# Forming the four weight sums of a seven-product down projection in DRAM, during the attention stages, instead of beside the products

## The chip, the cores and the metric

The kernel runs on one core of a Trainium2 chip. The metric is the device time of one execution in microseconds (us), lower is better. The kernel before took 995.37 us, the median of three runs (993.64 to 995.89).

## The reference, cut to what matters

One layer of a hybrid diffusion backbone on 512 latent tokens (D = 1024) with 256 context tokens. Modulated RMSNorm, a combined input projection, a short convolution branch, a bidirectional gated linear attention of four heads, sigmoid gates, an output projection, then a squared-ReLU MLP, a residual add and a last RMSNorm:

```python
sh1, sc1, ga1, sh2, sc2, ga2 = jnp.split(mod_lat, N_MOD, axis=-1)   # silu(c) @ w_ada + b_ada
o_lat = gla_bidir(ql, kl, vl, gfl, gbl, s_f, s_b)
y_lat = mixer_merge(x_a, b_a, c_a, r, gate_a, gate_b, o_lat, ...)
x = x + ga1 * (y_lat @ w_o)
x = x + ga2 * sq_relu_mlp(modulate(x, g_norm2, sh2, sc2), w_up, w_down)   # square(relu(h @ w_up)) @ w_down
return rmsnorm(x, g_final)
```

The change is about `w_down` alone: a 512x4096 matrix times a 4096x1024 one.

## The kernel before, in words

Everything is fp32. A matmul is made of three fp32r products (`mm3`): each operand is split into a high part (a cast on ScalarE) and a low part (a subtract on VectorE, `split`). Weights are streamed in tiles of 128x1024 (512 KB): `weights()` takes one of four `raw` buffers (NRAW), loads it by SyncE's queue, and splits it into `hi` and `lo`, five buffers each. `Stream` runs a plan of all weight tiles, three ahead of their use: v, q, then x_a, c, b (and q) for the convolution branch, ga, co, r, gb, go, wo, up and dn. The names of tiles follow: `r_co` is the raw tile, `h_co` and `l_co` its parts, `ps_co` the PSUM tile.

The stages: keys and the first modulation, then `projections()`, whose 57 steps are interleaved one by one with the steps of the attention of the four heads (`all_attention`), to about 453 us; `gates()` (r and gb, eight steps each); go, wo and up; from 815.4 us the down projection; then the last norm.

`second_mods()` sums the remaining modulation rows (`ada_sum`): eight loads of `w_ada` (tile `wa`, 512 KB, in the same four raw buffers) for one row of 1024, two `scalar_tensor_tensor` into `acc` on VectorE for each. It runs beside the projection steps from step MODS_FROM = 44 on, and beside the gates. `ada_rows` then splits the sum (`ah`, `al`) and spreads it over the partitions by matmuls into `ps_ar`.

The down projection is a seven-product scheme of Strassen's kind. The 4096x1024 weights are four quarters, `quarter(j, hf, p)`: half j of the rows, half hf of the columns, in eight tiles p. Product n takes eight blocks of 12 matmuls: a left part (`left_parts`: `aph`, `apl` from `ug`) and a weight tile. Four of the seven weights are sums of quarters. Before, tiles p of the sums stand in SBUF (`t_raw`, in four `big` buffers): product 1 loads quarter (0,0) there and splits it; products 2, 3 and 6 each add one more quarter on top of the same tile by an accumulating DMA on GpSimd's queue (`added`, L1056), after the split of the product before. Products 0, 4 and 5 use the raw ring: 0 and 4 a plain load, 5 a plain load (L1064) and then an accumulating DMA on top of it in the same raw tile.

GpSimd's queue also sets a few constants and loads: `lrf` and `lpb` memsets in each head (L610, L611), the v bias `vb` (L802), `acc` memsets and bias rows (L725, L726), `g` (L766). SyncE's queue holds the weight loads, in the plan's order, and the stores of the output rows.

Of the kernel before, what the change touches and what calls it, by code (L numbers as in the profile page):

```python
# [8 lines left out]
F32 = mybir.dt.float32  # L9
F32R = mybir.dt.float32r  # L10
# [3 lines left out]
ALU = mybir.AluOpType  # L14

P = 128
# [15 lines left out]
NFF = D_FF // P  # L32
# [7 lines left out]
NBLK = 36  # L40
NKEEP = 16
MODS_FROM = 44
UP_ORDER = [16 * j + 4 * g + i for g in range(4) for j in range(2) for i in range(4)]
TABLES = "natural_log_exp_and_others"

# [2 lines left out]
def hybrid_block_kernel(  # L48
# [6 lines left out]
    nc = tc.nc  # L55
    x, ctx, w_ada, w_in = x[0], ctx[0], w_ada[0], w_in[0]
    conv_w, w_conv_out, w_gla_out, w_o = conv_w[0], w_conv_out[0], w_gla_out[0], w_o[0]
    w_up, w_down, b_in, b_ada, out = w_up[0], w_down[0], b_in[0], b_ada[0], out[0]

    const = es.enter_context(tc.tile_pool(name="const", bufs=1))  # L60
    wp = es.enter_context(tc.tile_pool(name="wp", bufs=NW))
    kp = es.enter_context(tc.tile_pool(name="kp", bufs=NKEEP))
    sp = es.enter_context(tc.tile_pool(name="sp", bufs=4))
    pp = es.enter_context(tc.tile_pool(name="pp", bufs=8, space=bass.MemoryType.PSUM))

    bp = tc.alloc_tile_pool(name="bp", bufs=NBLK)

# [23 lines left out]
    def kblk(name, dt=F32):  # L91
        return kp.tile([P, 512], dt, tag="kb", name=name)

    def big(name):

        t = [kp.tile([P, 4, 512], F32R, tag="big", name=f"{name}_{i}", bufs=4) for i in range(2)]
        return t, [t[k // 4][:, k % 4, :] for k in range(KT)]
# [4 lines left out]
    def raw_tile(name):  # L102
        return wp.tile([P, 1024], F32, tag="raw", name=name, bufs=NRAW)

    def pinned(ins):
        tc.keep_in_program_order(ins)

    def split(src, hi, lo):
        act.copy(out=hi, in_=src)
        dve.tensor_tensor(out=lo, in0=src, in1=hi.bitcast(F32), op=ALU.subtract)  # L110

    def parts_of(name, src):
        got = blk(name + "h", F32R), blk(name + "l", F32R)
        split(src, *got)
        return got

    def weights(name, src):

        raw = raw_tile("r_" + name)
        a, b = src.shape[1], src.shape[2]  # L120
        nc.sync.dma_start(out=raw.rearrange("p (a b) -> p a b", a=a), in_=src)
        hi = wp.tile([P, 1024], F32R, tag="hi", name="h_" + name)
        lo = wp.tile([P, 1024], F32R, tag="lo", name="l_" + name)
        split(raw, hi, lo)
        return hi.rearrange("p (a b) -> p a b", a=a), lo.rearrange("p (a b) -> p a b", a=a)

    def parted(name, src):

        hi = wp.tile([P, 1024], F32R, tag="hi", name="h_" + name)
        lo = wp.tile([P, 1024], F32R, tag="lo", name="l_" + name)  # L130
        split(src, hi, lo)
        return hi.rearrange("p (a b) -> p a b", a=2), lo.rearrange("p (a b) -> p a b", a=2)

    def mm3(ps, lh, ll, rh, rl, start, stop, late=False, more=False):


        pe.matmul(ps, lh, rh, start=start, stop=False, skip_group_check=more)
        for l, r in ((ll, rh), (lh, rl)) if late else ((lh, rl), (ll, rh)):
            pe.matmul(ps, l, r, start=False, stop=stop and r is (rl if late else rh), skip_group_check=more)
# [4 lines left out]
    def rows(w, k0, c0):  # L144
        return w[k0 * P:(k0 + 2) * P, c0:c0 + 512].rearrange("(k p) c -> p k c", p=P)
# [49 lines left out]
    for m in range(MT):  # L195
        t = (kblk(f"x_{m}_0"), kblk(f"x_{m}_1"))
# [6 lines left out]
    def key_raw(k):  # L203
        wr = blk(f"wk_{k}")
        nc.sync.dma_start(out=wr, in_=w_in[k * P:(k + 1) * P, C_K:C_K + 512])
        return wr
# [91 lines left out]
    def constants():  # L298

        ps = psum("ps_vb")  # L300
        pe.transpose(out=ps[:, 0:97], in_=vec_b, identity=ident[:97, :97])
        dve.tensor_copy(out=col_b, in_=ps[:, 0:97])

        a2h, a2l = blk("a2h", F32R), blk("a2l")
        act.copy(out=a2h, in_=a2)
        dve.tensor_tensor(out=a2l, in0=a2, in1=a2h.bitcast(F32), op=ALU.subtract)
        dve.tensor_scalar(out=a2l, in0=a2l, scalar1=m_2, scalar2=None, op0=ALU.mult)
        dve.scalar_tensor_tensor(out=a2s, in0=a2h.bitcast(F32), scalar=m_01, in1=a2l, op0=ALU.mult, op1=ALU.add)
# [13 lines left out]
    _, h_hi = big("hh")  # L322
    _, h_lo = big("hl")
# [61 lines left out]
    for s in range(2):  # L385
        dve.tensor_copy(out=lr_sel[:, 64 * s:64 * s + 48].rearrange("p (i r) -> p i r", i=3),
                        in_=sel[:, 16 * s:16 * s + 16].unsqueeze(1).to_broadcast([P, 3, RANK]))
# [35 lines left out]
    for k in range(KT):  # L423
        if k == 3:
            constants()
        if k + 2 < KT:
            key_raws[k + 2] = key_raw(k + 2)
            mod_w[k + 2] = [ada_raw(k + 2, q) for q in range(2)]
            key_weights(k + 2)
        elif k + 2 == KT:  # L430
            for m in range(MC):
                t = (blk(f"c_{m}_0"), blk(f"c_{m}_1"))
                for hf in range(2):
                    nc.sync.dma_start(out=t[hf], in_=ctx[m * P:(m + 1) * P, hf * 512:(hf + 1) * 512])
                c_tok.append(t)
        st, sp_ = k == 0, k == KT - 1
        if k % 4 == 3:
            low_rank_products(ps_lr, h_f32, k - 3)
        if k == KT - 1:
            lr_parts = low_rank_parts(ps_lr, SEQ)  # L440
        for h in range(HEADS):
            if h == 0 and k + 1 < KT:
                sm = mod_rows(k + 1)
            if h == 2 and k + 1 < KT:
                with tc.high_priority(offset=60):
                    mod_cols(k + 1, sm)
                    latent_h(k + 1)
            mm3(ps_k[h], wk[k][0][:, h * P:(h + 1) * P], wk[k][1][:, h * P:(h + 1) * P], h_hi[k], h_lo[k], st, sp_, st)
        mm3(ps_q0, wq[0][:, k, :], wq[1][:, k, :], h_hi[k], h_lo[k], st, sp_)

    class Stream:

# [31 lines left out]
    plan += [("wo", rows(w_o, 2 * g, 512 * hf)) for hf in range(2) for g in range(KT // 2)]  # L484
    plan += [("up", cols(w_up, f * P)) for f in UP_ORDER]
    plan += [("dn", lambda n=n, p=p: down_weights(n, p)) for n in range(7) for p in range(NFF // 4)]
# [263 lines left out]
    def all_attention():  # L750
        for h in range(HEADS):
            yield from attention(h)
# [3 lines left out]
    def second_mods():  # L756
        yield from ada_sum(3)
        ps = psum("ps_ac")
        for k in range(KT):
            pe.matmul(ps[:, k:k + 1], ada[3][k // 4][:, (k % 4) * P:(k % 4 + 1) * P], ones[:, 0:1], start=True, stop=True)  # L760
        dve.tensor_copy(out=sh2, in_=ps[:, 0:KT])
        yield
        yield from ada_rows(4)
        for hf in range(2):
            g2 = blk("g2")
            nc.gpsimd.dma_start(out=g2, in_=g_norm2[0][hf * 512:(hf + 1) * 512].partition_broadcast(P))  # L766
            dve.scalar_tensor_tensor(out=ada[4][hf], in0=ada[4][hf], scalar=1.0, in1=g2, op0=ALU.add, op1=ALU.mult)
        yield from ada_rows(2)
# [125 lines left out]
            yield  # L894
        pinned(nc.scalar.preload_act_table_set(TABLES))

    att, mods = all_attention(), second_mods()
    for i, _ in enumerate(projections()):
        next(att, None)
        if i >= MODS_FROM:  # L900
            next(mods, None)
    for _ in att:
        next(mods, None)
    for _ in gates():
        next(mods, None)
    for _ in mods:
        pass


# [33 lines left out]
    _, h2_hi = big("h2h")  # L943
    _, h2_lo = big("h2l")
# [97 lines left out]
    def left_parts(n, b):  # L1042
# [2 lines left out]
        got = [mp.tile([P, 512], F32R, tag="ap" + i, name=f"ap{i}_{n}_{b}", bufs=3) for i in "hl"]  # L1045
        split(src, *got)
        return [t.rearrange("p (a m c) -> p a m c", a=2, m=2) for t in got]

    t_big = [kp.tile([P, 4, 512], F32, tag="big", name=f"t_{i}", bufs=4) for i in range(4)]
    t_raw = [t_big[p // 2][:, 2 * (p % 2):2 * (p % 2) + 2, :] for p in range(8)]  # L1050

    def quarter(j, hf, p):
        return rows(w_down, 16 * j + 2 * p, 512 * hf)

    def added(dst, src):
        nc.gpsimd.dma_start(out=dst, in_=src, accum_op=ALU.add)  # L1056

    def down_weights(n, p):

        flat = t_raw[p].rearrange("p a b -> p (a b)")  # L1060
        if n in (0, 4, 5):
            raw = raw_tile(f"r_dn{n}")
            r3 = raw.rearrange("p (a b) -> p a b", a=2)
            nc.sync.dma_start(out=r3, in_=quarter(*{0: (1, 0), 4: (1, 1), 5: (0, 1)}[n], p))  # L1064
            if n == 5:
                added(r3, quarter(1, 1, p))
            return parted("dn", raw)
        if n == 1:
            nc.sync.dma_start(out=t_raw[p], in_=quarter(0, 0, p))
        else:  # L1070
            added(t_raw[p], quarter(*{2: (0, 1), 3: (1, 1), 6: (1, 0)}[n], p))
        return parted("dn", flat)

    for f in UP_ORDER[EARLY:]:
        relu_sq(f, project("up", h2))
# [68 lines left out]
    for m in range(2):  # L1144
        t = mp.tile([P, 512], F32, tag="tmp", name="w", bufs=1)
# [77 lines left out]
```

## Time and profile before

| what | value |
|---|---|
| runs | 993.64, 995.37, 995.89 us, median 995.37 |
| the profiled execution | 996.37 us, span 994.6 us |
| mean granted TensorE clock | 0.993 of full speed |
| TensorE busy | 959.4 us (96%) |
| VectorE, ScalarE, GpSimd busy | 636.3, 487.7, 73.3 us |
| DMA, HBM read | 36.9% of the 16 engines' span on SyncE's queue, 10.5% on GpSimd's; 128.89 MB |

TensorE is busy for nearly the whole span, so what matters is in which stage it is not, outside of the first 30 us. Shares of other engines, and of the DMA queues, are averages over stages that differ much, and are to be read by stretch of time.

### The profile page before, as it was taken

To read this page: it belongs to the slowest core of one execution; us is meant where nothing else is said; L and a number is where in the kernel's file an instruction comes from. 1 tells how busy PE (TensorE), PEld (TensorE's weight loads), DVE (VectorE), ACT (ScalarE), POOL (GpSimd) and SP (SyncE) were. 2 spreads that over 40 slices of the span, in tenths; PEclk is the share of its full clock that TensorE was granted. 3 is DMA by queue.
4 is the path that set the end of the run, shared out by engine and by line. 5 is a ranking of instruction groups with operands and counts; after the bars stand their busy time and mean duration, and the time that the engine had idled before them with its cause. 6 is when DMAs were issued, how large, how long until landed. Compare 5 with 4: busy or idle time off the path is not lost.

```text
span 994.6 us, 13293 instructions
## 1 busy us (share of the span) xinstructions
PE 959.4 (96%) x4999; PEld 779.6 (78%) x4999; DVE 636.3 (64%) x1076; ACT 487.7 (49%) x862; POOL 73.3 (7%) x99
## 2 busy tenths in 40 slices
PE   3999999999999999999999999999999999999786
PEld 2768888778888888788888888888888888888565
DVE  5466676887688769857573554855322236898586
ACT  4466454645655564724533323554443446564452
POOL 7000000000000010000000000000000002340200
PEclk9999999999999999999999999999999999999898
DMA  9780112333232325626675244257333359998931
GB/s 274 230 286 1 47 51 85 85 85 85 64 86 71 99 64 156 183 64 176 184 210 150 85 158 118 63 147 234 88 105 90 111 175 268 162 202 216 223 78 43
DMA packets 154993, 131.85 MB, mean 133 GB/s; under 512 B 6373, under 2 KB 125265, under 8 KB 154929
## 3 DMA queue, kind: packets, MB, share of 16 engines
q1 hardware_dynamic: 144240, 111.30, 36.9%
q0 software_dynamic: 10112, 18.65, 10.5%
q10 hardware_dynamic: 576, 1.05, 0.3%
q8 instruction: 39, 0.64, 0.3%
q14 instruction: 26, 0.20, 0.1%
HBM read 128.89 MB, written 2.10 MB: 132 GB/s over the span
## 4 chain that ended last, share of the span: by engine, by line
PE 91%; DMA 4%; DVE 2%; SPq 1%; ACT 1%; issue 0%; DVEq 0%; ACTq 0%; POOLq 0%
PE ps_up L79 16%; PE ps_v L79 7%; PE ps_co L79 5%; PE ps_b L79 5%; PE ps_y L79 4%; PE ps_c L79 4%; PE ps_go L79 4%; PE ps_da L79 4%; PE ps_ga L79 4%; PE ps_xa L79 4%; PE ps_r L79 4%; PE ps_gb L79 4%; DMA r_dn<-in_w_down_dram 3%; PE ps_db L79 3%; PE ps_k L79 3%; PE ps_dc L79 2%
## 5 line engine op out<-in xcount | busy, mean ns | idle before, releaser
L79 DVE TENSOR_TENSOR l_up<-r_up,h_up 128x1024 fp32r<-128x1024 f32 x32 | 39.2, 1224 | 83.5 <-ACT h_up L79 83.5
L79 PE MATMUL ps_up<-h2h,l_up 128*128 128x512 f32 x232 | 90.3, 389 | 0.0
L79 PE MATMUL ps_up<-h2l,h_up 128*128 128x512 f32 x232 | 90.3, 389 | 0.0
L79 PE MATMUL ps_up<-h2h,h_up 128*128 128x512 f32 x232 | 90.3, 389 | 0.0
L79 ACT CAST h_up<-r_up 128x1024 fp32r<-128x1024 f32 x32 | 33.6, 1053 | 78.6 <-PE ps_up L79 67.9
L79 ACT CAST aph<-ug 128x512 fp32r<-128x512 f32 x56 | 34.7, 620 | 48.4 <-PE ps_da L79 19.6
L79 DVE TENSOR_TENSOR l_dn<-r_dn,h_dn 128x1024 fp32r<-128x1024 f32 x24 | 29.3, 1223 | 39.2 <-ACT h_dn L79 39.1
L79 DVE SCALAR_TENSOR_TENSOR acc<-wa,silu_c,acc 128x512 f32<-128x512 f32 x64 | 45.4, 747 | 11.9 <-DMA wa<-in_w_ada_dram 11.8
L79 PEld LDWEIGHTS ps_up<-h2h,l_up 128*128 128x128 f32 x232 | 43.5, 188 | 9.1
L79 PEld LDWEIGHTS ps_up<-h2h,h_up 128*128 128x128 f32 x232 | 43.5, 188 | 9.0
L79 PEld LDWEIGHTS ps_up<-h2l,h_up 128*128 128x128 f32 x232 | 43.5, 188 | 9.0
L79 DVE TENSOR_TENSOR apl<-ug,aph 128x512 fp32r<-128x512 f32 x56 | 38.5, 687 | 10.5 <-ACT aph L79 10.3
L79 ACT CAST h_dn<-r_dn 128x1024 fp32r<-128x1024 f32 x24 | 25.2, 1048 | 39.1 <-DMA r_dn<-in_w_down_dram 20.2
L79 PE MATMUL ps_da<-h_dn,apl 128*128 128x512 f32 x96 | 39.1, 407 | 4.7 <-DVE apl L79 4.7
L79 PE MATMUL ps_da<-h_dn,aph 128*128 128x512 f32 x96 | 38.8, 404 | 3.1 <-ACT aph L79 3.1
L79 DVE TENSOR_TENSOR l_dn<-t,h_dn 128x1024 fp32r<-128x1024 f32 x32 | 39.0, 1220 | 3.4 <-ACT h_dn L79 3.4
L79 PE MATMUL ps_da<-l_dn,aph 128*128 128x512 f32 x96 | 38.6, 402 | 0.0
L1056 POOL DMA_DIRECT2D t<-in_w_down_dram x24 | 28.7, 1195 | 69.8 <-DVE l_dn L79 69.8
L79 ACT CAST h_dn<-t 128x1024 fp32r<-128x1024 f32 x32 | 33.5, 1048 | 0.0
L79 PEld LDWEIGHTS ps_da<-h_dn,apl 128*128 128x128 f32 x96 | 18.4, 192 | 11.0 <-DVE apl L79 6.7
L79 PE MATMUL ps_v<-h_v,hh 128*128 128x512 f32 x64 | 26.0, 406 | 0.0
L79 PE MATMUL ps_co<-yah,h_co 128*128 128x512 f32 x64 | 25.7, 402 | 0.0
(457 smaller groups left out, 2814.8 us busy)
## 6 DMA issues: line engine op xcount, KB each, us to landing
wa<-in_w_ada_dram SPq DMA_DIRECT2D x32, 512.0 KB, 4.2
r_up<-in_w_up_dram SPq DMA_DIRECT2D x32, 512.0 KB, 3.9
r_dn<-in_w_down_dram SPq DMA_DIRECT2D x24, 512.0 KB, 5.4
t<-in_w_down_dram POOLq DMA_DIRECT2D x24, 512.0 KB, 6.8
wa<-in_w_ada_dram SPq DMA_DIRECT2D x32, 256.0 KB, 4.6
r_v<-in_w_in_dram SPq DMA_DIRECT2D x8, 512.0 KB, 5.1
r_xa<-in_w_in_dram SPq DMA_DIRECT2D x8, 512.0 KB, 3.9
r_c<-in_w_in_dram SPq DMA_DIRECT2D x8, 512.0 KB, 3.9
```

The costliest lines, as they stand in the source:

```text
L79: ins = op(*args, **kwargs)
L1056: nc.gpsimd.dma_start(out=dst, in_=src, accum_op=ALU.add)
```

## The change

Four DRAM tiles of eight parts, `t_sum[i][p]`, hold the sums. A generator, `weight_sums()`, issues 64 DMAs on GpSimd's queue, each of 512 KB from DRAM to DRAM: 16 copies of quarters (0,0) and (0,1) into t0 and t1, 16 adds on top of them, then copies of t0 into t2 and eight adds, copies of t2 into t3 and eight adds: 32 copies and 32 adds. Before each stands a copy of one element (`tick`) that reads the low part of the weight tile split last (`latest`), so that a DMA is not issued before that split. One such pair follows each step of `projections()` but the first (56 pairs), the last eight follow steps of `gates()`. Products 2, 3, 5 and 6 then load the finished sums by `weights()`, as products 0, 1 and 4 load quarters; `added`, `parted`, `t_big` and `t_raw` are gone.

```diff
+SUMS = (0, 1)
+    dp = es.enter_context(tc.tile_pool(name="dp", bufs=1, space=bass.MemoryType.DRAM))
 def weights(name, src):
         split(raw, hi, lo)
+        latest[0] = lo
-    def parted(name, src):
...
+    t_sum = [[dp.tile([P, 2, 512], F32, tag=f"t{i}_{p}", name=f"t{i}_{p}") for p in range(NFF // 4)] for i in range(4)]
+    tick = const.tile([1, 1], F32, name="tick")
+    def weight_sums():
+        groups = range(NFF // 4)
+        todo = [(i, p, quarter(0, i, p), False) for p in groups for i in range(2)]
+        todo += [(i, p, quarter(i, 1, p), True) for p in groups for i in range(2)]
+        for i, j, hf in ((2, 1, 1), (3, 1, 0)):
+            todo += [(i, p, t_sum[(0, 2)[i - 2]][p], False) for p in groups]
+            todo += [(i, p, quarter(j, hf, p), True) for p in groups]
+        for i, p, src, add in todo:
+            pinned(nc.gpsimd.tensor_copy(out=tick, in_=latest[0][0:1, 0:1].bitcast(F32)))
+            pinned(nc.gpsimd.dma_start(out=t_sum[i][p], in_=src, **({"accum_op": ALU.add} if add else {})))
+            yield
+    def down_weights(n, p):
+        if n in (2, 3, 5, 6):
+            return weights("dn", t_sum[{2: 0, 3: 2, 5: 1, 6: 3}[n]][p])
+        return weights("dn", quarter(*{0: (1, 0), 1: (0, 0), 4: (1, 1)}[n], p))
...
     for i, _ in enumerate(projections()):
         next(att, None)
+        for _ in range(SUMS[min(i, len(SUMS) - 1)]):
+            next(sums, None)
         if i >= MODS_FROM:
             next(mods, None)
     for _ in gates():
         next(mods, None)
+        next(sums, None)
...
-    def added(dst, src):
-        nc.gpsimd.dma_start(out=dst, in_=src, accum_op=ALU.add)
-    def down_weights(n, p):
-        flat = t_raw[p].rearrange("p a b -> p (a b)")
-        if n in (0, 4, 5):
-            raw = raw_tile(f"r_dn{n}")
-            r3 = raw.rearrange("p (a b) -> p a b", a=2)
-            nc.sync.dma_start(out=r3, in_=quarter(*{0: (1, 0), 4: (1, 1), 5: (0, 1)}[n], p))
-            if n == 5:
-                added(r3, quarter(1, 1, p))
-            return parted("dn", raw)
-        if n == 1:
-            nc.sync.dma_start(out=t_raw[p], in_=quarter(0, 0, p))
-        else:
-            added(t_raw[p], quarter(*{2: (0, 1), 3: (1, 1), 6: (1, 0)}[n], p))
-        return parted("dn", flat)
```

The order on TensorE, VectorE and ScalarE stays as it was, but for names. It moves on the two queues.

SyncE, end of the down projection, before: the last plain loads of product 5 (their adds stand on GpSimd's queue), then the stores; product 6 has nothing here.

```order
L1064 DMA r_dn_8226<-in_w_down_dram 128x2x512 [waits DMASW5_49,DVE_49]
L1064 DMA r_dn_8249<-in_w_down_dram 128x2x512 [waits DMASW6_49,DVE_49]
L1123 DMA out_dram<-x_0_0_5645 128x512 [waits DMAHW3_49,DVE_49]
L1123 DMA out_dram<-x_1_0_5650 128x512 [waits DMAHW5_49,DVE_49]
L1193 DMA out_dram<-x_2_0_5655 128x512 [waits DMAHW7_49,DVE_49]
```

After: the sums t1 (product 5) and t3 (product 6) are loaded here, two stores stand between the loads of product 6.

```order
L125 DMA r_dn<-t_6_696 128x1024 [waits DMAHW5_49,DVE_49]
L125 DMA r_dn<-t_7_697 128x1024 [waits DMAHW6_49,DVE_49]
L125 DMA r_dn<-t_0_706 128x1024 [waits DMASW3_49,DMAHW7_49,DVE_49,Activation_49]
L1128 DMA out_dram<-x_0_0_5808 128x512 [waits DVE_49]
L125 DMA r_dn<-t_1_707 128x1024 [waits DMASW4_49,DMAHW0_49,DVE_49,Activation_49]
L125 DMA r_dn<-t_2_708 128x1024 [waits DMAHW1_49,DMASW5_49,DVE_49]
L1128 DMA out_dram<-x_1_0_5813 128x512 [waits DVE_49]
L125 DMA r_dn<-t_3_709 128x1024 [waits DMAHW2_49,DMASW6_49,DVE_49]
```

In this place eight loads have come in for the accumulating DMAs, and the stores of x_0 and x_1 have seven and five loads of product 6 behind them.

GpSimd, around the second `vb` load, before:

```order
L611 MEMSET lpb 128x512 [waits DVE_49,Activation_49]
L802 DMA vb_1326<-in_b_in_dram 128x512 [waits DMASW6_49,PE_49]
L610 MEMSET lrf 128x512 [waits DVE_49,PE_49]
L611 MEMSET lpb 128x512 [waits DMASW5_49,PE_49,Activation_49]
L610 MEMSET lrf 128x512 [waits DVE_49,PE_49]
```

After: `l_v` is the low part of a v weight tile.

```order
L466 COPY tick<-l_v 1x1 [waits Pool_49]
L467 DMA t_2_692<-in_w_down_dram 256x1x512 [waits DMASW3_49]
L466 COPY tick<-l_v 1x1 [waits DVE_49,Pool_49]
L467 DMA t_3_685<-in_w_down_dram 256x1x512 [waits DMASW4_49]
L827 DMA vb_1375<-in_b_in_dram 128x512 [waits DMASW5_49,PE_49]
L466 COPY tick<-l_q 1x1 [waits DVE_49,Pool_49]
```

The bias load now stands behind two pairs of tick and add, each of which waits for a split of a v tile.

GpSimd, at the end of the attention and the start of the r gate, before: memsets and bias rows of one modulation row, then `g`.

```order
L725 MEMSET acc_4306 128x512 [waits DMAHW0_49,DMAHW3_49,DVE_49,PE_49]
L725 MEMSET acc_4307 128x512 [waits DMAHW6_49,DVE_49,Activation_49]
L726 DMA acc_4306<-in_b_ada_dram 1x16x32 [waits DMASW1_49,Pool_49]
L726 DMA acc_4307<-in_b_ada_dram 1x16x32 [waits DMASW2_49,Pool_49]
L766 DMA g_4824<-in_g_norm_dram 128x512 [waits DMASW3_49,PE_49]
L766 DMA g_4827<-in_g_norm_dram 128x512 [waits DMASW4_49,DVE_49]
L725 MEMSET acc_4830 128x512 [waits DVE_49]
L725 MEMSET acc_4831 128x512 [waits DVE_49]
```

After:

```order
L750 MEMSET acc_4447 128x512 [waits DMAHW0_49,DMAHW3_49,DVE_49,PE_49]
L750 MEMSET acc_4448 128x512 [waits DMAHW6_49,DVE_49,Activation_49]
L751 DMA acc_4447<-in_b_ada_dram 1x16x32 [waits DMASW6_49,Pool_49]
L751 DMA acc_4448<-in_b_ada_dram 1x16x32 [waits DMASW7_49,Pool_49]
L466 COPY tick<-l_r 1x1
L467 DMA t_5_711<-t_5_703 16x8192 [waits DMASW0_49]
L466 COPY tick<-l_r 1x1 [waits Pool_49]
L467 DMA t_6_712<-t_6_704 16x8192 [waits DMASW1_49]
L466 COPY tick<-l_r 1x1 [waits Pool_49]
L467 DMA t_7_713<-t_7_705 16x8192 [waits DMASW2_49]
L466 COPY tick<-l_r 1x1 [waits DVE_49,Pool_49]
L467 DMA t_0_706<-in_w_down_dram 256x1x512 [waits DMASW3_49]
```

Three copies of t2 into t3 have gathered behind the memsets of `acc`, and the adds that finish t3 follow, each after a split of an r tile.

## Rows read from the trace of the kernel before

**Rows 1.** The page, busy time of TensorE, share of the span, instructions.

```profile
PE 959.4 (96%) x4999; PEld 779.6 (78%) x4999; DVE 636.3 (64%) x1076; ACT 487.7 (49%) x862; POOL 73.3 (7%) x99
```

**Rows 2.** Waits of TensorE, 60 to 810 us: us, times, longest.

```profile
PE ps_sd L79 <- ACT h_c L79: 0.5, 1, 0.5
```

**Rows 3.** Waits of TensorE, 815 to 995 us: us, times, longest.

```profile
PE ps_da L79 <- DVE apl L79: 4.7, 4, 2.6
PE ps_da L79 <- ACT aph L79: 3.1, 1, 3.1
PE ps_dd L79 <- DVE apl L79: 2.3, 1, 2.3
```

**Rows 4.** Chain that ended last, the first product (n = 0): start, length, pieces.

```profile
815.52 22.31 PE ps_db L79 x96
```

**Rows 5.** Timeline of TensorE, first matmuls of products 4, 5 and 6.

```profile
904.59 0.40 PE L79 MATMUL ps_db<-h_dn,aph 128*128 128x512 f32 x1
...
927.29 0.50 PE L79 MATMUL ps_da<-h_dn,aph 128*128 128x512 f32 x1
...
960.75 0.39 PE L79 MATMUL ps_dd<-h_dn,aph 128*128 128x512 f32 x1
```

**Rows 6.** Chain that ended last, 895 to 995 us, its transfers.

```profile
916.57 9.18 DMA r_dn<-in_w_down_dram
...
927.00 8.42 DMA r_dn<-in_w_down_dram
...
937.82 7.12 DMA r_dn<-in_w_down_dram
945.50 7.00 DMA r_dn<-in_w_down_dram
```

**Rows 7.** Windows in product 5: width, PE PEld DVE ACT POOL busy, PEclk, DMA share, GB/s.

```profile
940.00:945.00 5.00, 4.15 (x12) 3.29 (x13) 4.49 (x12) 4.83 (x14) 0.00 (x0) 0.59 0.98 213
```

**Rows 8.** Windows, product 2, same columns.

```profile
860.00:882.00 22.00, 22.00 (x96) 17.87 (x95) 21.95 (x27) 13.37 (x19) 9.54 (x8) 1.00 0.90 155
```

**Rows 9.** The page, DMA queues and issues: KB each, us to landing.

```profile
q1 hardware_dynamic: 144240, 111.30, 36.9%
q0 software_dynamic: 10112, 18.65, 10.5%
...
r_dn<-in_w_down_dram SPq DMA_DIRECT2D x24, 512.0 KB, 5.4
```

**Rows 10.** Windows in the r gate's stage, columns as in rows 7.

```profile
455.00:460.00 5.00, 5.00 (x26) 4.15 (x25) 2.98 (x6) 3.30 (x6) 0.00 (x0) 1.00 0.88 258
460.00:465.00 5.00, 5.00 (x25) 4.10 (x24) 1.86 (x3) 2.38 (x3) 0.00 (x0) 1.00 0.96 302
465.00:470.00 5.00, 5.00 (x26) 4.13 (x24) 5.00 (x7) 2.15 (x3) 0.55 (x1) 1.00 0.50 162
470.00:475.00 5.00, 5.00 (x25) 4.14 (x24) 3.83 (x6) 1.68 (x2) 0.53 (x1) 1.00 1.03 290
```

**Rows 11.** Timeline of VectorE and TensorE, r gate's stage.

```profile
457.77 1.22 DVE L79 TENSOR_TENSOR l_r<-r_r,h_r 128x1024 fp32r<-128x1024 f32 x1 [1.01 <-ACT h_r L79]
...
472.21 1.22 DVE L79 TENSOR_TENSOR l_r<-r_r,h_r 128x1024 fp32r<-128x1024 f32 x1
474.48 1.41 DVE L79 SCALAR_TENSOR_TENSOR acc<-wa,silu_c,acc 128x512 f32<-128x512 f32 x2 [1.04 <-DMA wa<-in_w_ada_dram]
...
487.31 1.29 DVE L79 TENSOR_TENSOR al<-acc,ah 128x512 fp32r<-128x512 f32 x2
...
488.83 0.48 PE L79 MATMUL ps_ar<-ah,ones_r 128*128 128x512 f32 x1
```

**Rows 12.** Windows, last attention steps, columns as in rows 7.

```profile
385.00:410.00 25.00, 25.00 (x150) 19.79 (x149) 23.28 (x44) 16.91 (x32) 0.00 (x0) 1.00 0.79 230
```

**Rows 13.** Timeline of VectorE, the second vb.

```profile
118.70 3.72 DVE L79 TENSOR_TENSOR l_v<-r_v,h_v 128x1024 fp32r<-128x1024 f32 x3
...
131.15 0.69 DVE L79 TENSOR_TENSOR v<-ps_v,vb 128x512 f32<-128x512 f32 x1
```

More of the change, by code (lines that the diff above doesn't have):

```diff
@@ L115, in parts_of @@
         return got
+    latest = [None]
     def weights(name, src):
@@ L124, in weights @@
         split(raw, hi, lo)
+        latest[0] = lo
         return hi.rearrange("p (a b) -> p a b", a=a), lo.rearrange("p (a b) -> p a b", a=a)
-    def parted(name, src):
[L129 to L132, printed above, removed]
     def mm3(ps, lh, ll, rh, rl, start, stop, late=False, more=False):
@@ L449, in hybrid_block_kernel, with quarter @@
         mm3(ps_q0, wq[0][:, k, :], wq[1][:, k, :], h_hi[k], h_lo[k], st, sp_)
+    t_sum = [[dp.tile([P, 2, 512], F32, tag=f"t{i}_{p}", name=f"t{i}_{p}") for p in range(NFF // 4)] for i in range(4)]
+    tick = const.tile([1, 1], F32, name="tick")
+    def quarter(j, hf, p):
+        return rows(w_down, 16 * j + 2 * p, 512 * hf)
+    def weight_sums():
[13 more added lines that the diff above has]
+        return weights("dn", quarter(*{0: (1, 0), 1: (0, 0), 4: (1, 1)}[n], p))
     class Stream:
@@ L895, in gates @@
         pinned(nc.scalar.preload_act_table_set(TABLES))
-    att, mods = all_attention(), second_mods()
+    att, mods, sums = all_attention(), second_mods(), weight_sums()
     for i, _ in enumerate(projections()):
         next(att, None)
+        for _ in range(SUMS[min(i, len(SUMS) - 1)]):
+            next(sums, None)
         if i >= MODS_FROM:
@@ L905, in hybrid_block_kernel @@
         next(mods, None)
+        next(sums, None)
     for _ in mods:
+        pass
+    for _ in sums:
         pass
@@ L1047, in left_parts @@
         return [t.rearrange("p (a m c) -> p a m c", a=2, m=2) for t in got]
[L1049 to L1053, printed above, removed]
-    def added(dst, src):
-        nc.gpsimd.dma_start(out=dst, in_=src, accum_op=ALU.add)
-    def down_weights(n, p):
-        flat = t_raw[p].rearrange("p a b -> p (a b)")
-        if n in (0, 4, 5):
-            raw = raw_tile(f"r_dn{n}")
-            r3 = raw.rearrange("p (a b) -> p a b", a=2)
-            nc.sync.dma_start(out=r3, in_=quarter(*{0: (1, 0), 4: (1, 1), 5: (0, 1)}[n], p))
-            if n == 5:
-                added(r3, quarter(1, 1, p))
-            return parted("dn", raw)
-        if n == 1:
-            nc.sync.dma_start(out=t_raw[p], in_=quarter(0, 0, p))
-        else:
-            added(t_raw[p], quarter(*{2: (0, 1), 3: (1, 1), 6: (1, 0)}[n], p))
-        return parted("dn", flat)
     for f in UP_ORDER[EARLY:]:
```

## The prediction

> **What bounds the kernel now.** I read the busy times first, then what TensorE waits for in the stages, then the chain of waits through the down projection, and last the DMA share in short windows where the change puts new transfers. TensorE is busy for 959.4 us, 96% of the span [rows 1]. From 60 to 810 us it waits once, for 0.5 us [rows 2]; no stage there can become faster by better transfers, but each can become slower. Its later waits lie in the down projection: for apl 4.7 us, for aph 3.1 us and 2.3 us for apl again [rows 3].
>
> The first of the seven products goes through in 22.31 us [rows 4], and products 1 to 3 keep that pitch. Products 4 and 5 together take 960.75 - 904.59 = 56.16 us [rows 5] where two full products take 2 x 22.31 = 44.62. So 11.54 us are lost. The chain says to what: through product 5 it runs over four transfers into r_dn of 9.18, 8.42, 7.12 and 7.00 us, one behind the other [rows 6]. These are the plain load and the add on top of it, in a ring of four buffers; the add can't begin before the load has landed. After these waits TensorE also ran at a granted clock of 0.59 for one window of 5 us [rows 7], which is in the 11.54 us.
>
> **The change, part by part**, against the profiled execution's 996.37 us, which stands 1.0 us above the median of the runs, 995.37.
>
> Product 5 loads a finished sum: one transfer in place of two in series. In this ring a plain load lands after 5.4 us at the median, with adds beside it [rows 9], and the adds are gone from this stage. A block of TensorE's work is 22.31 / 8 = 2.8 us, so four buffers cover 11 us. VectorE remains close behind: in product 2 it was busy 21.95 of 22.00 us, and TensorE still 22.00 [rows 8]; product 5 lacks the `ug` update that product 2 carries. So I take the whole loss away: **-11.5 us** (bounds -11.5 and -8, the latter if some of VectorE's waits come back as work).
>
> The 2.3 us in product 6 [rows 3] stay. That wait ends with an apl that stands on VectorE behind the outputs of product 5, and VectorE's order does not change: **0** (bounds -2.3 and +1). The stores that now stand between the loads of product 6 wait for values that VectorE writes ahead of the splits which release those very loads, so they hold nothing up: 0.
>
> Products 2, 3 and 6 lose their adds, which were hidden: TensorE had no wait in 0 to 4. Their 24 loads in place of 24 adds cost less of the rings: 0.
>
> The 64 transfers are the price. Queue q0 took 10.5% of 994.6 us for 18.65 MB, nearly all of it the 32 adds: 5.6 us for 1 MB, or **2.94 us of all 16 engines for an add** of 0.524 MB. Queue q1 took 36.9% for 111.30 MB, 3.30 us for 1 MB, 1.73 us for a load [rows 9]. These adds ended in SBUF. For one that ends in DRAM no row has a price; I bound it by 1.73 us, a plain load, and 5.9 us, twice the add, and take 2.94, as the same quarter is read by the same queue. A copy I take as a load. Where the rings are idle this is hidden. There are two crowded places.
>
> At 385 to 410 us the DMA share is 0.79 [rows 12], which leaves 0.21 x 25 = 5.2 us. The last two adds of t2 (5.9 us) and some three copies (5.2 us) come there. The 6 us too much move loads of co and wa that are issued well ahead; VectorE does not wait for wa in this stretch. **0** (bounds 0 and +3).
>
> At 455 to 475 us, in the r gate, the shares are 0.88, 0.96, 0.50 and 1.03 [rows 10]: 5 x (0.12 + 0.04 + 0.50 - 0.03) = 3.2 us idle. Here VectorE waits for wa already (1.04 us ahead of the acc at 474.48), and from there work in order leads to al, at 487.31 for 1.29 us, done at 488.6; TensorE wants it at 488.83 [rows 11]. This is a chain with 0.2 us to spare. Four adds of t3 are released in the stretch, each by an l_r, from the one at 457.77 to the one at 472.21 [rows 11]: 4 x 2.94 = 11.8 us, less 3.2 idle, 8.6. The fourth comes late enough that only half of it stands ahead of what al needs (-1.5): wa, the r tiles and al come **7 us** later, and TensorE waits for al that long (bounds 0, if packets of loads slip past adds, and 11.8). Nothing later gives this back, as no stage behind it has waits to save.
>
> As for the order in which the rings serve the two queues: the Trainium skill, "DMA: Bandwidth & Descriptors", section "Queues, rings and completion order", says that each DMA engine takes turns between the queues that it has work for, a whole packet at a time, so a load wanted at once has no precedence over a sum wanted 400 us later. By that rule the adds cost the loads their full time, 11.8 us, and the sum would be about 0. The rows above, with a share of 1.03 at most and 0.5 us of idle rings between, leave less than that.
>
> GpSimd's own steps: the second vb load now stands behind a tick on the v splits, which begin at 118.70 and last 3.72 us, and is used at 131.15 [rows 13]. That leaves 8.7 us for two issues and a landing: 0 (bounds 0 and +3). The lrf, lpb and acc memsets have as much room or more; a tick is one element.
>
> Sum: -11.5 + 7 = -4.5, so 991.9 for the profiled execution and **991 us** for the median.
>
> **The rivals.** About 0.2%, 2 us, is what a measurement of this kernel can tell from no change.
>
> *Hidden altogether.* The ticks spread the adds so well, or an add in DRAM costs so little (1.73 us: 4 x 1.73 - 3.2 = 3.7 us, of which less reaches al), that only 0 to 3.5 us come back: 984 to 987.9. For it: one wait of 0.5 us from 60 to 810 us [rows 2] shows how far ahead most loads are. Against it: the 0.2 us ahead of ps_ar.
>
> *All given back.* Each add costs the loads beside it its full time, idle rings or not, 11.8 us at al; or the 3 us at 385 to 410 and those at vb come besides my 7: 995.4 - 11.5 + 11.8 = 995.7, with spread 993.4 to 997.4. The first of these is the rule of the Trainium skill named above.
>
> *VectorE in the place of the DMA.* Its 21.95 busy us of 22.00 [rows 8] become the bound once nothing else is, in products 5 and 6, and 3 of the 11.5 us stay on top of my 7: 994.
>
> *Slower.* An add into DRAM occupies the rings for longer, as it must read and write DRAM. The place is the r gate, the price 3.5 adds less the 3.2 idle us. It decides at the price c where 3.5 c - 3.2 = 13.5, that is c = 4.8 us; with 5.9 the wait for al is 17.4 us and the time 995.4 - 11.5 + 17.4 = 1001. For it: no row has such an add. Against it: SBUF or DRAM, the same bytes go by the same queue.
>
> *Not done as said:* sums late for the products. The last add is issued near 490 us, product 2 wants t0 after 850. I give that nothing.
>
> **How the numbers follow.** Forecast, 988 to 993.4: 0.44. Hidden altogether: 0.18. All given back: 0.17. VectorE: 0.05. Slower: 0.16. So faster 0.44 + 0.18 = 0.62, same 0.17 + 0.05 = 0.22, slower 0.16. The range leaves out the far half of the slower case and a little of the hidden one: 984.5 to 997.5. The likeliest case's own range is 988 to 993.4.
>
> **What would show it.** After: products 4 and 5 at 22.3 us each, no r_dn in the chain there, no clock below 1.00; a wait of some 7 us of TensorE for al at ps_ar near 489 us, or for an r tile; DMA shares over 1.0 from 455 to 485; q0's share near 32 x 2.94 + 32 x 1.73 = 149 us of the span, 15%. I am wrong if product 5 still waits, if al is in time, or if the wait is in another stage: scores near 390 us, v near 131.

## The result, and the profile after

The changed kernel takes 1002.06 us (median of five, 1001.34 to 1005.91) where the kernel before takes 995.37 (993.64 to 996.53, five runs): a ratio of 1.0077, interval 1.0054 to 1.010. It is slower by 6.7 us, outside the range that was given. The profiled execution took 1002.8 us, with a span of 1001.0 us.

The down projection did what was forecast. The chain through it, start, length and pieces, in the kernel after:

```profile
923.72 22.32 PE ps_db L81 x96
946.03 22.31 PE ps_da L81 x96
```

Products 4 and 5 take 22.3 us each, and no transfer stands between them, where there were four [rows 6]. So the loss is ahead of it. This is where the stages begin (first matmul of each on TensorE, us, from the two traces):

| stage | before | after | later by | of which new in the stage ahead of it |
|---|---|---|---|---|
| ps_v | 68.2 | 69.3 | 1.1 | 1.1, the start-up |
| ps_ga | 343.6 | 344.8 | 1.2 | 0.1 |
| ps_co | 398.0 | 403.8 | 5.8 | 4.6 |
| ps_r | 453.3 | 466.1 | 12.8 | 7.0 |
| ps_go | 546.2 | 565.2 | 19.0 | 6.2 |
| ps_db | 815.4 | 834.3 | 18.9 | -0.1 |
| ps_dd | 960.7 | 968.2 | 7.5 | -11.4 |

Two losses came in: 4.6 + 7.0 = 11.6 us from 380 to 420 us, in the last attention steps (ga and co), and 6.2 us in the r gate. The 1.1 us at the start lies ahead of the first new transfer, and the starts of the other kernels below scatter by as much. What TensorE waits for in the kernel after, 60 to 1001 us (us, times, longest):

```profile
PE ps_sl L81 <- DVE kt L81: 6.8, 2, 5.0
PE ps_ar L81 <- ACT ah L81: 2.8, 1, 2.8
PE ps_dd L81 <- DVE apl L81: 1.6, 1, 1.6
PE ps_s L81 <- DVE vcl L81: 1.3, 1, 1.3
PE ps_sd L81 <- ACT h_c L81: 0.5, 1, 0.5
```

VectorE makes kt and vcl for the attention's matmuls. The waits for them are at two places, 1.8 + 1.3 us near 387 us and 5.0 us at 410 to 415; that for ah is in the r gate:

```profile
386.44 0.69 PE L81 MATMUL ps_sl<-qt,kt 128*64 128x64 f32 x16 [1.76 <-DVE kt L81]
388.72 0.58 PE L81 MATMUL ps_s<-vcl,kwh 128*128 128x256 f32 x1 [1.28 <-DVE vcl L81]
414.67 1.12 PE L81 MATMUL ps_sl<-qt,kt 128*64 128x64 f32 x16 [5.01 <-DVE kt L81]
```

The waits, 8.1 and 2.8 us, are less than the losses, 11.6 and 6.2. The rest is clock. Windows of the kernel after, columns as in rows 7:

```profile
380.00:385.00 5.00, 4.68 (x21) 3.55 (x19) 0.00 (x0) 2.19 (x5) 0.00 (x0) 1.00 0.77 200
385.00:390.00 5.00, 2.28 (x23) 2.02 (x24) 4.92 (x11) 3.78 (x11) 0.00 (x0) 0.81 0.01 3
390.00:395.00 5.00, 5.00 (x23) 4.38 (x23) 5.00 (x11) 1.64 (x2) 0.00 (x0) 0.84 0.68 204
...
410.00:415.00 5.00, 0.33 (x6) 0.33 (x8) 2.81 (x5) 4.27 (x8) 0.97 (x2) 0.70 0.81 258
415.00:420.00 5.00, 5.00 (x28) 4.04 (x25) 4.73 (x10) 5.00 (x9) 0.00 (x0) 0.61 0.85 261
```

After each of these waits TensorE runs for some us at a lower granted clock. Busy time times what is missing to 1.00 gives 0.19 x 2.28 + 0.16 x 5.00 + 0.30 x 0.33 + 0.39 x 5.00 = 3.3 us; with 8.1 us of waits that is 11.4 of the 11.6. In the r gate:

```profile
500.00:505.00 5.00, 2.19 (x12) 1.60 (x10) 3.47 (x5) 3.57 (x6) 5.00 (x9) 0.92 1.10 248
505.00:510.00 5.00, 4.99 (x12) 3.57 (x12) 1.00 (x2) 0.12 (x1) 0.09 (x1) 0.50 1.09 290
510.00:515.00 5.00, 5.00 (x24) 4.09 (x23) 0.93 (x1) 2.06 (x4) 0.00 (x0) 0.90 0.90 195
```

Here one window at 0.50, which is 1.2 GHz, and its neighbours cost 0.2 + 2.5 + 0.5 = 3.2 us; with the 2.8 us of wait that is 6.0 of the 6.2. What is late here is r_r, not wa. For wa VectorE waits 1.3 us in all between 470 and 510 us, and the last `acc` ahead of ah is done by 493.5. For r_r ScalarE sits in front of a cast:

```profile
489.83 1.05 ACT L81 CAST h_r<-r_r 128x1024 fp32r<-128x1024 f32 x1 [8.21 <-DMA r_r<-in_w_in_dram]
```

From there ScalarE and VectorE work off in their order what has piled up, and ah comes at 503.98. No run tests that chain by itself.

What holds kt is told by three engines' timelines. Twice GpSimd issues two adds of t2 within 3 us, and SyncE a load of r_co between them; the chain that ended last shows how long each of the two loads took:

```profile
372.82 1.11 POOL L467 DMA_DIRECT2D t<-in_w_down_dram  x1 [0.45 <-issue]
...
375.01 1.08 POOL L467 DMA_DIRECT2D t<-in_w_down_dram  x1 [0.20 <-issue]
...
395.65 1.00 POOL L467 DMA_DIRECT2D t<-in_w_down_dram  x1
...
398.11 1.00 POOL L467 DMA_DIRECT2D t<-in_w_down_dram  x1
```

```profile
374.10 8.63 DMA r_co<-in_w_conv_out_dram
...
397.49 13.14 DMA r_co<-in_w_conv_out_dram
```

Before, a load of r_co landed after 3.3 to 5.4 us; after, after 3.5 to 13.1. ScalarE and VectorE in the kernel after:

```profile
382.81 1.05 ACT L81 CAST h_co<-r_co 128x1024 fp32r<-128x1024 f32 x1 [7.79 <-DMA r_co<-in_w_conv_out_dram]
...
384.34 0.41 ACT L81 ACTIVATE qt<-lrb 128x256 f32<-128x256 f32 x1
...
410.70 1.04 ACT L81 CAST h_co<-r_co 128x1024 fp32r<-128x1024 f32 x1 [10.80 <-DMA r_co<-in_w_conv_out_dram]
```

```profile
385.08 0.69 DVE L81 TENSOR_TENSOR qt<-qt,q 128x512 f32<-128x512 f32 x1 [5.55 <-ACT qt L81]
```

No matmul wants the first of these tiles yet: ps_co begins at 403.8. But its cast stands in ScalarE's order ahead of the attention's exponentials (`qt`), whose inputs are ready. ScalarE sits for 7.79 us in front of the cast, VectorE 5.55 us in front of qt, and TensorE 1.76 us behind kt and 1.28 behind vcl. At the second place ScalarE sits for 10.80 us, and TensorE, behind kt, for 5.01. So some 5 to 6 us of ScalarE's wait do not reach TensorE; before, ScalarE sat 2.8 and 3.2 us in front of these casts and no matmul was late.

The rows of before that would have told this are the issues of the same two loads and their casts on ScalarE:

```profile
372.88 0.37 SPq L121 DMA_DIRECT2D r_co<-in_w_conv_out_dram  x1
...
391.38 0.37 SPq L121 DMA_DIRECT2D r_co<-in_w_conv_out_dram  x1
```

```profile
376.60 1.05 ACT L79 CAST h_co<-r_co 128x1024 fp32r<-128x1024 f32 x1 [2.81 <-PE ps_ga L79]
...
397.24 1.04 ACT L79 CAST h_co<-r_co 128x1024 fp32r<-128x1024 f32 x1 [3.20 <-PE ps_ga L79]
```

These loads were issued 3.7 and 5.9 us before their casts began, and a load landed after 3.3 to 5.4 us: little was in hand for a longer landing. One of the casts between them, at 386.92, waited 0.6 us for its load already.

### The profile page after: what moved, and what is told of

It reads as the page before. It is cut to its first block, busy times and chain, and to the rows that moved or that the text cites. A ratio compares the mean times of both kernels' runs of the same rounds, so it can differ in the third digit from the quotient of the medians.

```text
span 1001.0 us, 13478 instructions
## 1 busy us (share of the span) xinstructions
PE 963.0 (96%) x4999; PEld 783.9 (78%) x4999; DVE 637.0 (64%) x1076; ACT 487.8 (49%) x862; POOL 109.2 (11%) x195
## 3 DMA queue, kind: packets, MB, share of 16 engines
q0 software_dynamic: 12928, 35.43, 15.1%
## 4 chain that ended last, share of the span: by engine, by line
PE 90%; DMA 4%; DVE 3%; SPq 1%; ACT 1%; issue 1%; DVEq 0%; ACTq 0%
PE ps_up L81 16%; PE ps_da L81 7%; PE ps_v L81 7%; PE ps_b L81 4%; PE ps_y L81 4%; PE ps_c L81 4%; PE ps_db L81 4%; PE ps_go L81 4%; PE ps_xa L81 4%; PE ps_gb L81 4%; PE ps_co L81 4%; PE ps_r L81 4%; PE ps_ga L81 2%; PE ps_dc L81 2%; DMA r_co<-in_w_conv_out_dram 2%; PE ps_k L81 2%
## 5 line engine op out<-in xcount | busy, mean ns | idle before, releaser
L81 DVE TENSOR_TENSOR l_dn<-r_dn,h_dn 128x1024 fp32r<-128x1024 f32 x56 | 68.4, 1222 | 27.1 <-ACT h_dn L81 26.9
L81 ACT CAST h_dn<-r_dn 128x1024 fp32r<-128x1024 f32 x56 | 58.7, 1048 | 16.1 <-PE ps_up L81 16.1
L467 POOL DMA_DIRECT2D t<-in_w_down_dram x48 | 42.7, 905 | 3.8 <-issue 3.8
L81 PE MATMUL ps_r<-hh,h_r 128*128 128x512 f32 x64 | 26.4, 412 | 0.0
L81 PE MATMUL ps_r<-hh,l_r 128*128 128x512 f32 x64 | 25.8, 402 | 0.0
L81 PE MATMUL ps_r<-hl,h_r 128*128 128x512 f32 x64 | 25.7, 401 | 0.0
```

The lines of the kernel that those rows point to most:

```text
L81: ins = op(*args, **kwargs)
L467: pinned(nc.gpsimd.dma_start(out=t_sum[i][p], in_=src, **({"accum_op": ALU.add} if add else {})))
```

## The experiments

The theory: the down projection gains its 11.5 us, and adds beside loads that ScalarE or VectorE take in a fixed order, in front of attention work, take it away at two places. Rivals: 64 transfers cost wherever they are; part of the loss is in the loads of the sums; backlog rather than place. Times are medians; the ratio to the kernel before, run beside each, and its interval follow.

**No sums.** Products load plain quarters, `weight_sums` issues nothing.

```diff
-        for i, p, src, add in todo:
+        for i, p, src, add in ():
...
+        return weights("dn", quarter(*{0: (1, 0), 1: (0, 0), 2: (0, 1), 3: (1, 1), 4: (1, 1), 5: (0, 1), 6: (1, 0)}[n], p))
```

> The changed kernel with no sums formed at all: the 64 ticks and transfers are left out, and products 2, 3, 5 and 6 load plain quarters of w_down in their place (so their weights are not the sums). Theory (the down projection gains what was forecast and the 64 transfers take it away, at two places): 995.4 - 11.5, so 983 to 986 us, product 5 at 22.3 us, no wait for kt near 385 us and none at ps_ar. Rival (part of the loss is in the loads of the down projection or in their order): above 988 us.

984.29 us (984.16 to 984.57; 0.989, 0.9875 to 0.9904). TensorE's waits from 60 us on are two:

```profile
PE ps_dd L81 <- DVE apl L81: 1.6, 1, 1.6
PE ps_sd L81 <- ACT h_c L81: 0.5, 1, 0.5
```

From the first matmul of ps_db to the first of ps_dd it takes 133.9 us, as the changed kernel does, so loading the sums costs nothing there. So the down projection is worth what was forecast, and the 64 transfers cost 1002.1 - 984.3 = 17.8 us, the 11.6 and 6.2 of the table.

**All sums ahead of the modulation rows, two a step.**

```diff
-SUMS = (0, 1)
+SUMS = (0, 2)
```

> SUMS = (0, 2): the same 64 transfers, two a step, so that the last is issued by step 32, ahead of the modulation rows. Theory (it is the place that costs: adds beside the wa and r_co loads): 984 to 988 us, no wait for kt near 390 us, none at ps_ar. Rival (64 transfers in the attention cost the same wherever they stand): 999 us or more, with the waits moved to 100 to 300 us.

989.92 us (0.9945, 0.993 to 0.996), the same transfers in other places: 12 us of the 17.8 are gone, and the kernel is faster than before. The waits near 390 us and at ps_ar are gone. A new one came, of the same kind, near 205 us; ScalarE and TensorE, 200 to 250 us:

```profile
ACT h_c L81 <- DMA r_c<-in_w_in_dram: 9.4, 1, 9.4
```

```profile
PE ps_sl L81 <- DVE kt L81: 2.9, 1, 2.9
```

Eight adds are issued there between 164 and 175 us, because the splits that their ticks wait for come close together there (l_c, l_b and l_xa at 161.7, 162.9 and 164.9 us), and the DMA share is 0.99 to 1.21 from 165 to 195 us. SyncE took 13.7 us to issue the load ahead of this r_c. Neither figure of mine was hit: place decides most of it, and a crowd of adds makes a new place.

**Copies in place of the adds.**

```diff
-nc.gpsimd.dma_start(out=t_sum[i][p], in_=src, **({"accum_op": ALU.add} if add else {}))
+nc.gpsimd.dma_start(out=t_sum[i][p], in_=src, )
```

> The 32 adds issued as plain copies, in the same places (what is formed in DRAM is then a quarter, not a sum). Theory (the ring time of the adds beside r_co decides, 2.94 us for an add and 1.73 for a copy): loads of r_co land sooner, 990 to 997 us. Rival (the number of GpSimd's transfers or its ticks decides, not their time): 1000 to 1003 us.

987.76 us (0.9926, 0.9909 to 0.9942), below what the theory expected: 14.3 of the 17.8 us go with what an add takes beyond a copy, and not with the number of transfers. The other 3.5 us stay, with two waits for kt, 2.4 us together. The page's row of q0 (packets, MB, share) here, in the changed kernel and with no sums:

```profile
q0 software_dynamic: 8832, 35.43, 9.8%
```

```profile
q0 software_dynamic: 12928, 35.43, 15.1%
```

```profile
q0 software_dynamic: 1408, 1.87, 0.8%
```

64 copies and the small loads take 9.8% of 986.0 us, 96.6 us; without the 0.8% of 982.8 us that q0 takes with no sums, 7.9 us, a copy is 1.39 us. In the changed kernel q0 took 15.1% of 1001.0, 151.2 us, so an add is 1.39 + (151.2 - 96.6) / 32 = 3.1 us. The adds also bring more packets, so whether packets or time decide isn't told apart.

**Only the adds of t3 left in the gates.**

```diff
-SUMS = (0, 1)
+SUMS = (0,) + (2,) * 28 + (0,)
```

> 56 transfers two a step, by step 28, and only the eight adds of t3 left where they are, in the gates. Theory: the loss near 390 us (11.6 us by the two profiles) is gone, the one at ps_ar (about 6 us) stays: 988 to 992 us. Rival (the loss at ps_ar is only the earlier delay carried on): 984 to 987 us. Rival (place does not matter): 999 us or more.

993.15 us (991.37 to 997.42; 0.9981, 0.9962 to 1.000), 3.2 us above the kernel with all sums early. The wait at ps_ar stays, the two near 390 and 410 us are gone, the one near 205 us is there as with two a step. The expectation had left that one out, and so the figure lies above it.

**Four adds of t2 alone**, those beside the co loads, with four copies ahead of them. Products load plain quarters here and in the kernels of single adds below.

```diff
-        for i, p, src, add in todo:
+        for k, (i, p, src, add) in enumerate(todo):
+            if k not in (*range(36, 40), *range(44, 48)):
+                yield
+                continue
+            src = quarter(1, 1, p)
```

> As e1_no_sums (products load plain quarters), but with the four adds of t2 that stand beside the co loads (steps 47 to 50, about 373 to 399 us in the changed kernel) and four copies some 60 us ahead of them; the other 56 ticks and transfers are left out. Theory (two adds in flight beside one r_co load hold its cast, which stands at the head of ScalarE's queue ahead of the attention's qt): the waits for kt near 390 and 410 us come back nearly whole, 984.3 + 8 to 12, so 992 to 996 us. Rival (the loss needs the backlog of all 64 transfers): 984 to 986 us.

992.71 us (990.73 to 994.8; 0.9975, 0.9957 to 0.9993): four of the 64 transfers, with their copies, cost 8.4 us. TensorE's waits there and two of the windows:

```profile
PE ps_sl L81 <- DVE kt L81: 4.6, 1, 4.6
...
PE ps_s L81 <- DVE vcl L81: 0.9, 1, 0.9
```

```profile
405.00:410.00 5.00, 1.41 (x7) 0.81 (x5) 1.46 (x2) 2.59 (x6) 0.00 (x0) 0.90 1.08 343
410.00:415.00 5.00, 3.96 (x23) 3.27 (x24) 5.00 (x11) 4.97 (x9) 0.00 (x0) 0.50 0.50 154
```

5.5 us of waits, and the window at 0.50 behind them. No backlog of 64 transfers is needed.

**The first pair, the second pair, and two single adds.** The line above with `(36, 37, 44, 45)`, `(38, 39, 46, 47)` and `(37, 39, 45, 47)`.

> As e5_four_adds, but with the first two of its four adds alone (about 372 and 375 us; products load plain quarters). Theory (each pair of adds holds the r_co load beside it, and each held load costs by itself): the wait for kt of 4.6 us near 410 us goes, that near 390 us stays, 984.3 + 1 to 3, so 985 to 988 us. Rival (the first pair starts a backlog that is paid later): 990 to 993 us as with four.

> As e5_four_adds, but with its third and fourth adds alone (one behind the other, after the splits of the third and fourth co tile, about 390 to 397 us; products load plain quarters). Theory (each pair costs by itself, so that e5's loss of 8.4 us is the 1.3 us of the first pair and the rest of the second): the wait for kt near 405 us is there, 984.3 + 5 to 8, so 989 to 993 us. Rival (the second pair costs only on top of the delay that the first has left): 984 to 987 us.

> As e5_four_adds, but with the second and the fourth of its adds alone, so that no load of r_co meets two. Theory (one add is 2.9 us of the rings, and the cast of r_co was waited for by 0.6 to 2.9 us already, so one add holds it for some 3 us, which the slack ahead of the scores takes up for the most part): 984 to 987 us. Rival (any add beside r_co or wa costs its full ring time, and half of it again in clock): 988 to 993 us.

First pair 985.54 us (0.9898, 0.987 to 0.9926), second pair 989.41 (0.9947, 0.9926 to 0.9968), two singles 984.01 (0.9882, 0.9854 to 0.991). Against no sums that is 1.3, 5.1 and nothing that can be told. The pairs together, 6.4 us, make most of the 8.4. Each of the three kernels has two adds, so their number does not decide. Adds that do not meet cost nothing here, though each is 3.1 us of the rings: the two are issued 18.5 us apart. How long loads of r_co took, with singles and with the second pair:

```profile
DMA to landing us min/median/max: 3.5/4.7/6.1
```

```profile
DMA to landing us min/median/max: 3.6/3.7/11.5
```

ScalarE's longest wait for r_co was 2.9 us with no sums, 5.6 with the first pair and 8.9 with the second; TensorE's longest wait there was none, 1.0 and 2.8. So here, too, some 5 to 6 us do not reach TensorE. That the delay passes by ScalarE's order is read from the traces; no kernel was run with the cast elsewhere in that order.

**The eight adds in the gates alone**, their copies in the first steps.

```diff
+            if k not in (*range(0, 8), *range(56, 64)):
+                yield
+                continue
+            i, p, src = 3, k % 8, quarter(1, 0, k % 8)
```

> As e1_no_sums (products load plain quarters), with eight copies in the first steps and the eight adds of t3 in the gates alone. Theory (the chain wa, acc, ah, al, ps_ar has 0.2 us to spare, and the adds beside its loads cost by themselves what the profile of the changed kernel shows there, a wait of 2.8 us and a half-clock stretch): 988 to 992 us. Rival (the loss there comes from the backlog of the copies of t3 and the earlier stalls): 984 to 986 us.

990.08 us (986.01 to 993.27, seven runs; 0.9956, 0.9934 to 0.9979): 5.8 us by themselves, without copies near them or earlier stalls. These adds are issued one by one, 3.6 to 5.6 us apart, and cost all the same; the DMA share there is 0.88 to 1.03 in three of four windows without them [rows 10]. The profiled execution is the fastest of the seven, 986.01 us, and still shows the wait, 60 to 980 us:

```profile
PE ps_ar L81 <- ACT ah L81: 1.5, 1, 1.5
```

**Two a step, then one.** `SUMS = (0,) + (2,) * 21 + (1,)`.

> The changed kernel with two transfers a step to step 21 and one a step from there to step 43, so that all are issued ahead of the modulation rows, and the adds of t2 and t3 mostly one a step. Theory (pairs of adds beside a load that ScalarE waits for are what costs, as near 230 us in e2_two_a_step, 5.6 us): 984 to 987 us if the adds of t2 there come singly, 989 to 991 if a pair still meets r_c. Rival (64 transfers before step 44 cost 5 to 6 us however they are spread): 989 to 991 us with waits at another place.

989.41 us (0.9932, 0.9904 to 0.996). Both lines of the expectation allowed this figure, so it tells nothing apart by the time (the wait of two a step that it places near 230 us stands near 205). Its trace has the same crowd near 165 us and one wait for kt of 3.1 us near 205 us, as with two a step.

**The last 21 transfers in go and up**, one a step as in the change to step 43.

```diff
+SUMS = (0,) + (1,) * 43 + (0,)
...
     for _ in gates():
         next(mods, None)
-        next(sums, None)
...
         ps = project("go", og)
+        next(sums, None)
...
         relu_sq(f, project("up", h2))
+        next(sums, None)
```

> The changed kernel with its one transfer a step to step 43, no transfer in steps 44 to 56 nor in the gates, and the last 21 in the go and up stages (one a weight tile). Theory (the places beside wa cost): 984 to 987 us, no wait for kt near 385 us or at ps_ar, none in the up stage, whose loads are issued further ahead of use. Rival (the transfers cost wherever they are): waits in go, wo or up, 990 us or more.

985.47 us (0.9894, 0.9863 to 0.9926). All 64 transfers, with the sums used, and 1.2 us above none at all. Against the expectation the up stage has a short wait, once more at ps_ar, where the last modulation row is summed. The chain leads to it from a load of r_up that took 15.3 us, by ScalarE's cast of it:

```profile
PE ps_ar L81 <- ACT ah L81: 0.7, 1, 0.7
...
PE ps_ar L81 <- DVE al L81: 0.4, 1, 0.4
```

**The sum of product 5 alone in DRAM.** The kernel before, its adds in SBUF for products 2, 3 and 6 kept; eight copies and eight adds in steps 1 to 16.

```diff
+        todo = [(p, j) for j in range(2) for p in range(NFF // 4)]
+        for p, j in todo:
+            pinned(nc.gpsimd.tensor_copy(out=tick, in_=latest[0][0:1, 0:1].bitcast(F32)))
+            pinned(nc.gpsimd.dma_start(out=t_sum[p], in_=quarter(j, 1, p), **({"accum_op": ALU.add} if j else {})))
+            yield
...
-            nc.sync.dma_start(out=r3, in_=quarter(*{0: (1, 0), 4: (1, 1), 5: (0, 1)}[n], p))
-            if n == 5:
-                added(r3, quarter(1, 1, p))
+            nc.sync.dma_start(out=r3, in_=t_sum[p] if n == 5 else quarter(*{0: (1, 0), 4: (1, 1)}[n], p))
```

> The kernel before, with its adds in SBUF for products 2, 3 and 6 as they were, and the sum of product 5 alone formed in DRAM: eight copies and eight adds, one a step, in steps 1 to 16. Theory (only product 5's add was not hidden, and single transfers in the early steps cost nothing): 995.5 - 11.5, 983 to 986 us, as without any sums. Rival (the adds in SBUF would now hold up product 6, whose add waits for splits that come sooner; or early steps cost): 988 us or more.

984.83 us (983.96 to 986.54, six runs; 0.9892, 0.9864 to 0.992), as fast as with no sums at all, and faster than the kernel before and the changed one. Products 4 and 5 in its chain:

```profile
904.90 22.31 PE ps_db L82 x96
927.21 22.31 PE ps_da L82 x96
```

## Why the prediction was wrong

- **Product 5, -11.5 us: right.** The chain shows 22.3 us for each of the two products, and the kernel with no sums is 11.1 us below the median before, 995.37.
- **Product 6, 0: nearly.** Its wait fell from 2.3 [rows 3] to 1.6 us. **VectorE in the place of the DMA** did not come: TensorE waits for VectorE 1.6 us in the whole down projection, where it was 7.0, and VectorE was busy 19.5 and 20.3 us of 22.3 in products 4 and 5.
- **The price of a transfer: right.** 2.94 us forecast for an add into DRAM, 3.1 measured; 1.73 forecast for a copy, 1.39 measured; q0's share 15%, as forecast. The rival that reached the other side rested on an add of 4.8 us or more, so the time came out slower by another way than the one I had priced.
- **380 to 420 us, taken as 0 with a bound of +3: this is the step that failed.** It cost 11.6 us, 8.1 in waits and 3.3 in clock. I argued that the loads of co and wa "are issued well ahead; VectorE does not wait for wa in this stretch". The second holds, but does not decide. The first does not hold: the two loads of r_co were issued 3.7 and 5.9 us ahead of their casts on ScalarE, took 8.6 and 13.1 us beside two adds each, and the scores' exponentials stand behind those casts. I asked who needs the tile, not who stands behind the instruction that takes it. The kernels with four adds alone (8.4 us) and with pairs and singles show the loss without the other transfers. The prediction did name "scores near 390 us" as a sign of being wrong, and it came.
- **The r gate, 7 us: right in place, and in size partly by luck** (6.2 in the traces, 5.8 by itself). The wait is 2.8 us, not 7, and 3.2 us of lower clock stand behind it, where I had expected no clock below 1.00. The chain that I priced goes by wa and acc; what was late was r_r, with ah behind its casts on ScalarE.
- **Served in turns.** The rule of the Trainium skill ("DMA: Bandwidth & Descriptors", "Queues, rings and completion order") gave 11.8 us for the adds in the gates, all of their ring time; the trace stays below with 6.2 us. That an urgent load has no precedence agrees with the r_co loads of 8.63 and 13.14 us beside sums wanted 400 us later.
- **vb, lrf, lpb, acc, 0: right.** TensorE has no new wait from 60 to 380 us.

With 11.6 in place of 0 and 6.2 of 7, my sum would have been 996.37 - 11.5 + 11.6 + 6.2 = 1002.7 against 1002.8 measured. That it is so close is luck too: the 1.1 us lost in the start-up and 1.1 us gained behind product 5 cancel.

## What to carry to other kernels

Before a transfer is put beside others "for nothing", look for each load it will meet at the engine that takes it: if the load is issued only a little longer before that instruction than it takes to land, everything behind the instruction in that engine's order is late too, wanted or not. Space such transfers so that they do not meet: here two adds 18.5 us apart cost nothing, and two within 3 us cost 1.3 or 5.1 us. In the r gate, where the rings are busier, 3.6 to 5.6 us apart were not enough. And move only what was not hidden: of 32 adds in the down projection, eight were on the path, and moving those alone gave the whole gain with a quarter of the transfers.

## What was not expected of the hardware

A wait of TensorE cost more than itself: in the changed kernel 1.2 us of clock behind the 3.1 us of waits near 387 us, 2.0 behind the 5.0 at 410 to 415, and 3.2 behind the 2.8 in the r gate. Shorter ones need not: with copies in place of the adds two waits for kt, 2.4 us together, left the clock at 1.00 from 380 to 420 us.

The scatter of the times differs too: with no sums four runs lie within 0.4 us, with the eight adds in the gates seven runs lie 7.3 us apart. No run shows why.
